# A hybrid decoder step on one core: weight pieces in a ring of four, the last tiles of a pass by quarters, and the base blocks' transposed copy on the vector engine

## The chip, the cores and the metric

One Trainium2 chip, one of its cores. Times are device microseconds (us) of one execution of the whole program. The engines are PE (TensorE, matrix products), DVE (VectorE), ACT (ScalarE), POOL (GpSimd) and SP (SyncE, which here only issues transfers). Each engine works through its own instructions in a fixed order and waits on semaphores where an instruction needs another engine's result. All five can run at once.

## The reference

One layer of a hybrid decoder for a prompt of 1024 tokens and 8 x 8 sample tokens, D_MODEL = 1024. One input projection feeds three groups of heads, whose outputs are joined by one output projection; then an MLP and a gated per-layer embedding.

```python
h = rmsnorm(x, lw['g_mix'])
proj = h @ lw['w_in']
p_rw, p_cv, p_sb = jnp.split(proj, [RW_PROJ, RW_PROJ + 3 * CONV_DIM], axis=-1)
o_rw, wkv_new, shift_new = rwkv7_mixer(p_rw, shift_prev, wkv_prev, lw)
...
q, k, v = [t.reshape(B, T, SB_HEADS, HEAD_DIM) for t in jnp.split(p_sb, 3, axis=-1)]
q = rmsnorm(q, lw['q_gain'])
k = rmsnorm(k, lw['k_gain'])
...
o_sb = stick_breaking(q, k_all, v_all, past_len, lw['sb_bias']).reshape(B, T, SB_DIM)
mixed = jnp.concatenate([o_rw.astype(x.dtype), o_cv.astype(x.dtype), o_sb.astype(x.dtype)], axis=-1)
x = x + mixed @ lw['w_out']
h2 = rmsnorm(x, lw['g_mlp'])
x = x + jnp.square(jax.nn.relu(h2 @ lw['w_up'])) @ lw['w_down']
gate = jax.nn.sigmoid(rmsnorm(x, lw['g_ple']) @ lw['w_ple_gate'])
x = x + gate * (p @ lw['w_ple_proj'])
```

The RWKV group is a recurrence over tokens, `s = s * w + (s a) b^T + v k^T`, `y = s r`, for each of 4 heads. The stick-breaking attention of 8 heads weighs each earlier key with `sigmoid(z)` times the product of `sigmoid(-z)` over the keys between.

## The kernel before

Products are made in fp32 accuracy from two rounded halves: an operand x is split into hi (a copy in the rounded type) and lo (x - hi), and each product is three matmuls, hi by hi, lo by hi and hi by lo. So each weight piece that arrives (tile `wr`, a DMA on SP) is cast by ACT (`wh`, L158) and subtracted by POOL or DVE (`wl`, L159) before PE can use it. `Weights.load` does this for the first stages: RWKV (256 or 128 columns at a time, over all 1024 rows), short conv, and the q, k and v projections of attention (512 columns, as two loads of 512 rows). `wh` and `wl` are two buffers each of a whole load, and `wr` two of one piece of 128x1024.

Stages in the order of the program:

1. Norm and transposes (0 to 45 us), then the RWKV projections (`gemm_t`, L169 to L171) for two pairs of heads j. For the recurrence, each chunk of 64 tokens (prompt) or 8 (sample) gives a triangular matrix: PE makes the products (L260), DVE masks them (`LT`, L262), a DMA lays them out in memory (`l_s`).
2. `wkv_base` inverts the diagonal blocks of these matrices. It loads them (`base_Z`, L278) with a block on each partition, and DVE then runs a loop of two dependent operations for each row (L285 multiplies, L287 adds): 62 operations for the prompt's 32x32 blocks on 128 partitions, 30 for the sample's 16x16 blocks on 16. ACT adds a transposed copy (L288), and SP stores both to `t_s` (L289), from where the later products are loaded as `TT`. The prompt's call stands after the projections of the second pair, the sample's at the head of `wkv_sample_chunk`, which runs at 450 to 580 us.
3. Three passes over eight 128-token tiles make v, q and k (PE at L889), then the prompt's recurrence chunks fill in between. In a pass a tile's 24 matmuls sum into one of two PSUM banks; ACT copies it out (`nat`, L839). In the v pass ACT and POOL split it (`spl`, L850 and L851) and SP stores it (`v_s`, L852), and the plain rows go to the output (L844). The two last tiles (i0 = 6) share the stage with `sample_rows`, which sums the 64 sample rows in one of the same two banks; ACT copies them out in two parts (`nats`, L825 and L826). `spl`, `nats` and the later `st` tiles share one ring of four buffers (tag "st").
4. Short conv, the sample's recurrence chunk and attention A (the first half of the queries), together with the first output projections `out_proj` (L1122 to L1124, groups of twelve matmuls, each group added by DVE at L1424). In attention PE makes the scores (L942, L943), DVE runs the scan (`keep`, L951) and the weighting (`beta`, L953), PE transposes the weights (L971), ACT and DVE split them (`wth`, `wtl`), PE makes the values (L981, L982), and DVE adds the two halves of `o` (L985).
5. Attention B with out_proj and MLP as filling work (from about 597 us), decode attention, the rest of the MLP and the embedding (to the end). PE is full in most of it.

The order on each engine isn't written by hand: the program is written stage by stage, and a list scheduler with a simulated timeline orders each engine's instructions, with `tc.high_priority()` and `tc.issue_after(...)` as hints. So an edit in one place moves instructions elsewhere.

Of the kernel before, what the change touches and what calls it, by code (L numbers as in the profile page):

```python
# [22 lines left out]
F32R = mybir.dt.float32r  # L23
# [25 lines left out]
def hybrid_step(ctx: ExitStack, tc: tile.TileContext, I, O):  # L49
    nc = tc.nc  # L50
    V, S, G, PE, SP = nc.vector, nc.scalar, nc.gpsimd, nc.tensor, nc.sync
# [4 lines left out]
    def f(t):  # L56
        return t.bitcast(F32)
# [36 lines left out]
    l_s = dram.tile([16, 4, 64, 64], F32, name="l_s"), dram.tile([1, 4, 64, 64], F32, name="l_s1")  # L94
    t_s = dram.tile([2, 16, 4, 2, 32, 32], F32, name="t_s"), dram.tile([4, 1, 4, 2, 16, 16], F32, name="t_s1")
# [41 lines left out]
    def P1(name, i=0):  # L137
        return par[:, col[name] + i:col[name] + i + 1]
# [4 lines left out]
    class Weights:  # L143
        def __init__(self, pool):
            self.pool = pool

        def load(self, src, nk=8, ncol=256, tag="w", sub=None):
            wh = self.pool.tile([128, nk * ncol], F32R, name="wh", tag=tag + "h", bufs=2)
            wl = self.pool.tile([128, nk * ncol], F32R, name="wl", tag=tag + "l", bufs=2)
            wh3, wl3 = (w[:, :nk * ncol].rearrange("p (k c) -> p k c", k=nk) for w in (wh, wl))  # L150
            step = max(1, 1024 // ncol)
            for k0 in range(0, nk, step):
                n = min(step, nk - k0)
                raw = self.pool.tile([128, 1024], F32, name="wr", bufs=2)
                r3 = raw[:, :n * ncol].rearrange("p (k c) -> p k c", k=n)
                SP.dma_start(r3, src[k0 * 128:(k0 + n) * 128, :].rearrange("(k p) c -> p k c", p=128))
                flat = slice(k0 * ncol, (k0 + n) * ncol)
                S.copy(wh[:, flat], raw[:, :n * ncol])  # L158
                (sub or (G, G))[k0 // step % 2].tensor_sub(wl[:, flat], raw[:, :n * ncol], f(wh[:, flat]))  # L159
            return wh3, wl3  # L160

    def gemm_t(ps, w, m, x, t0, n, nk=8):

        wh, wl = w
        xh, xl = x
        c = slice(m * 128, m * 128 + 128)
        for k in range(nk):
            a, b = xh[k // 4][:, k % 4, t0:t0 + n], xl[k // 4][:, k % 4, t0:t0 + n]
            PE.matmul(ps[:, :n], wh[:, k, c], a, start=(k == 0), stop=False)  # L169
            PE.matmul(ps[:, :n], wh[:, k, c], b, start=False, stop=False)  # L170
            PE.matmul(ps[:, :n], wl[:, k, c], a, start=False, stop=(k == nk - 1))  # L171

    w_in = I["w_in"][0]
    W = Weights(wpool)
# [6 lines left out]
    for i in range(9):  # L181
# [4 lines left out]
        xt, r = xts[i]  # L186
# [24 lines left out]
    for name, n in rows:  # L211
        src = I[name]
# [56 lines left out]
    def wkv_base(pool, nc_, BS, l_s, t_s, tags=("Z", "X", "Q"), bufs=(1, 1, 1)):  # L269
        na = 64 // BS  # L270
        np_ = nc_ * 4
        P_ = slice(0, na * np_)
        Z = pool.tile([128, BS, BS], F32, name="base_Z", tag=tags[0], bufs=bufs[0])
        X = pool.tile([128, 2, BS, BS], F32, name="base_X", tag=tags[1], bufs=bufs[1])
        Q = pool.tile([128, BS * BS // 4], F32, name="base_Q", tag=tags[2], bufs=bufs[2])
        blocks = l_s.rearrange("c h (a r) (b t) -> a b (c h) r t", a=na, b=na)
        for a in range(na):
            SP.dma_start(Z[a * np_:(a + 1) * np_], blocks[a, a])  # L278
        G.memset(X[P_, 1], 0.0)
        G.memset(X[P_, 1].rearrange("p r t -> p (r t)")[:, 0:BS * BS:BS + 1], 1.0)  # L280

        for j in range(BS - 1):
            n, m = BS - 1 - j, j + 1
            q = Q[P_, 0:n * m].rearrange("p (r c) -> p r c", r=n)
            V.tensor_mul(q, Z[P_, j, m:BS, None].to_broadcast([na * np_, n, m]),  # L285
                         X[P_, 1, None, j, 0:m].to_broadcast([na * np_, n, m]))
            V.tensor_add(X[P_, 1, m:BS, 0:m], X[P_, 1, m:BS, 0:m], q)  # L287
        S.copy(X[P_, 0], X[P_, 1].rearrange("p r t -> p t r"))  # L288
        SP.dma_start(t_s.rearrange("a c h k r t -> (a c h) k r t"), X[P_])  # L289


# [97 lines left out]
    for j in range(2):  # L389
# [312 lines left out]

    def wkv_sample_chunk(bank):
        sp = kp
        wkv_base(kp, 1, 16, l_s[1], t_s[1], ("um", "GS", "um"), (2, 1, 2))
        bm = sp.tile([128, NB, 64], F32, name="bm")
        G.memset(bm, 1.0)
        for s in range(2):
# [89 lines left out]
    def gained(n, flat, r=128):  # L798

        out = sbp.tile([128, 512], F32, name="kg", tag="kg", bufs=2)[:r]  # L800
        G.tensor_mul(*(t.rearrange("p (g d) -> p g d", d=64) for t in (out, flat)),
                     gains[:r, n, None, :].to_broadcast([r, 8, 64]))
        return out

    def products(w):

        for k in range(8):
            hi, lo = (x[k // 4][:, k % 4] for x in w)
            for e, wt in ((0, hi), (0, lo), (1, hi)):
                yield hT[e][k // 4][:, k % 4], wt, k == 0 and e == 0 and wt is hi, k == 7 and e == 1  # L810

    def sample_rows(n, w):

        both = sbp.tile([128, 8, 128], F32R, name="both", tag="nat", bufs=3)
        for e in range(2):
            for g in range(2):
                G.tensor_copy(both[:, 4 * g:4 * g + 4, 64 * e:64 * e + 64], hT[e][g][:, :, NP:T])
        ps = gemm_sb()
        order = [(128, 0)] + [x for k in range(1, 8) for x in ((64, k - 1), (128, k))]
        order[-1:] = [(64, 7), (128, 7)]  # L820
        for m, k in order:
            PE.matmul(ps[:m], both[:, k, :m], w[m == 64][k // 4][:, k % 4], start=(m, k) == (128, 0),
                      stop=(m, k) == (128, 7))
        out, low = (sbp.tile([128, 512], F32, name=f"nats{e}", tag="st", bufs=4)[:64] for e in range(2))
        S.copy(low, ps[64:128])  # L825
        S.copy(out, ps[:64])  # L826
        G.tensor_add(out, out, low)
        if n < 2:
            normed(out, out, NS)
            out = gained(n, out, NS)  # L830
        SP.dma_start(new_s[n], out)
        if n:
            SP.dma_start(outs[n][1][0].rearrange("b j h d -> (b j) (h d)"), out)

    def project(n, ps, i0, nat, i):

        t0 = 128 * (i0 + i)
        flat = nat[:, i]
        S.copy(flat, ps)  # L839
        if n < 2:  # L840
            normed(flat, ps)
        if n:
            out = gained(n, flat) if n == 1 else flat
            SP.dma_start(outs[n][0][0, 0].rearrange("t h d -> t (h d)")[t0:t0 + 128, :], out)  # L844
        if n == 2:
            src = flat.rearrange("p (h d) -> p h d", h=8)
            for hf in range(2):
                hs = slice(4 * hf, 4 * hf + 4)
                spl = sbp.tile([128, 4, 128], F32R, name="spl", tag="st", bufs=4)
                S.copy(spl[:, :, 0:64], src[:, hs])  # L850
                G.tensor_sub(spl[:, :, 64:128], src[:, hs], f(spl[:, :, 0:64]))  # L851
                SP.dma_start(v_s[hs, i0 + i].rearrange("h p e -> p h e"), f(spl))  # L852
# [22 lines left out]
    for n in (2, 0, 1):  # L875
        cols = slice(SB0 + 512 * n, SB0 + 512 * n + 512)
        with tc.high_priority():
            w = tuple(zip(*(W.load(w_in[512 * g:512 * g + 512, cols], nk=4, ncol=512, sub=(G, V)) for g in range(2))))
        for i0 in range(0, 8, 2):
            if i0 == 6:  # L880
                sample_rows(n, w)
            nat = sbp.tile([128, 2, 512], F32, name="nat", tag="nat", bufs=3)
            ps, whole = [None, None], list(products(w))
            for i, part in ((0, whole[:12]), (1, whole[:12]), (0, whole[12:]), (1, whole[12:])) if i0 == 6 else (
                    (0, whole), (1, whole)):
                ps[i] = ps[i] or gemm_sb()
                t0 = 128 * (i0 + i)
                for x, wt, start, stop in part:
                    last = PE.matmul(ps[i], x[:, t0:t0 + 128], wt, start=start, stop=stop)  # L889
# [764 lines left out]
```

## Time and profile before

| | |
|---|---|
| median of 3 runs | 1691.3 us (1691.1 to 1693.27) |
| profiled execution | 1697.94 us, span 1695.9 us |
| mean granted PE clock | 0.988 of full speed |
| busy: PE, DVE, ACT, POOL | 96%, 62%, 47%, 41% |
| moved by DMA | 196.9 MB, 116 GB/s on average |

PE is the engine that is nearly always busy. A change can move the time through PE's idle stretches and its slow ones (the granted clock falls after a stretch of idleness), and through the amount of PE's work, which this change leaves alone. A row of a timeline gives the start, the duration, engine and line, the output and input tiles and their shapes; in brackets stands the engine's idle time before it and what ended that. For a row of several instructions (x3) the duration is the sum's. A row of the windows gives for each engine the busy time in that stretch and its instructions, then the granted clock, the share of the DMA engines and GB/s.

### The profile page before, as it was taken

What the parts mean: (1) busy time and instruction counts of PE and PEld (TensorE: products, weight loads), DVE (VectorE), ACT (ScalarE), POOL (GpSimd) and SP (SyncE); (2) the same over time, 40 slices, a digit from 0 to 9 for tenths busy, and PEclk for the clock granted to TensorE, in tenths of its full rate; (3) what the DMA queues carried; (4) which work ended last, traced back from release to release, by engine and by line L of the source; (5) the groups of instructions that cost most, each with busy time, mean ns of one, the idle gap of its engine ahead of it and who ended that gap; (6) DMA issues with size and microseconds to landing.
All of it is one profiled execution on the core that took longest, in us unless ns stands there. A gap on an engine that the chain in (4) does not pass through costs nothing.

```text
span 1695.9 us, 29332 instructions
## 1 busy us (share of the span) xinstructions
PE 1630.5 (96%) x11229; PEld 1431.9 (84%) x11229; DVE 1054.7 (62%) x1814; ACT 792.1 (47%) x1559; POOL 701.2 (41%) x777
## 2 busy tenths in 40 slices
PE   6999899999998899999999999999999999999998
PEld 5899677778897577888886778988999999999898
DVE  6266644545488679878753335277777677767432
ACT  6544235334267367566543444474444334437421
POOL 4122312123244563333434654366655455538210
PEclk9999999999999899999999999999999999999999
DMA  6044664544246644343344655322322322322211
GB/s 192 27 142 132 174 177 113 137 101 138 71 129 192 167 147 127 105 127 105 92 122 138 186 177 181 122 77 86 99 89 79 96 88 88 96 80 88 72 46 41
DMA packets 201533, 196.92 MB, mean 116 GB/s; under 512 B 58033, under 2 KB 161489, under 8 KB 201266
## 3 DMA queue, kind: packets, MB, share of 16 engines
q1 hardware_dynamic: 189394, 173.52, 34.0%
q0 software_dynamic: 5120, 16.78, 3.3%
q10 hardware_dynamic: 6880, 4.75, 1.1%
q8 instruction: 88, 1.44, 0.3%
q14 instruction: 51, 0.42, 0.1%
HBM read 158.03 MB, written 36.98 MB: 115 GB/s over the span
## 4 chain that ended last, share of the span: by engine, by line
PE 81%; DVE 8%; issue 3%; DMA 3%; ACT 2%; POOL 2%; SPq 1%; ACTq 0%; POOLq 0%; DVEq 0%
PE b L1122 13%; PE b L1124 13%; PE b L1123 13%; PE b L889 6%; PE b L1469 3%; PE b L1471 3%; PE b L1470 3%; PE b L169 3%; PE b L170 3%; PE b L171 3%; DVE keep L951 2%; PE b L971 1%; PE b L524 1%; PE b L981 1%; PE b L1247 1%
## 5 line engine op out<-in xcount | busy, mean ns | idle before, releaser
L1103 POOL TENSOR_TENSOR wl<-wr,wh 128x512 fp32r<-128x512 f32 x172 | 238.7, 1396 | 265.6 <-ACT wh L1102 243.2
L1102 ACT CAST wh<-wr 128x512 fp32r<-128x512 f32 x292 | 179.2, 622 | 298.1 <-PE b L1123 206.3
L1122 PE MATMUL b<-ah,wh 128*128 128x288 f32 (+1 forms) x768 | 254.7, 332 | 5.9 <-DVE x L1509 4.9
L1509 DVE TENSOR_TENSOR x<-b,x 128x288 f32<-128x288 f32 (+1 forms) x384 | 198.4, 528 | 97.0 <-PE b L1124 94.4
L1123 PE MATMUL b<-al,wh 128*128 128x288 f32 (+1 forms) x768 | 252.0, 328 | 0.0
L1124 PE MATMUL b<-ah,wl 128*128 128x288 f32 (+1 forms) x768 | 251.9, 328 | 0.0
L1122 PE MATMUL b<-nh,wh 128*128 128x512 f32 (+1 forms) x448 | 165.8, 371 | 4.4 <-DVE x L1509 1.5
L1123 PE MATMUL b<-nl,wh 128*128 128x512 f32 (+1 forms) x448 | 164.4, 368 | 0.2 <-DVE nl L1346 0.2
L1124 PE MATMUL b<-nh,wl 128*128 128x512 f32 (+1 forms) x448 | 164.2, 367 | 0.0
L1122 PEld LDWEIGHTS b<-ah,wh 128*128 128x128 f32 x768 | 144.6, 188 | 18.4 <-DVE x L1509 8.0
L1123 PEld LDWEIGHTS b<-al,wh 128*128 128x128 f32 x768 | 144.8, 188 | 10.2 <-issue 0.8
L1124 PEld LDWEIGHTS b<-ah,wl 128*128 128x128 f32 x768 | 144.6, 188 | 10.3
L169 PE MATMUL b<-h_hi,wh 128*128 128x384 f32 (+1 forms) x336 | 114.1, 340 | 3.3 <-ACT xs L345 1.3
L170 PE MATMUL b<-h_lo,wh 128*128 128x384 f32 (+1 forms) x336 | 112.6, 335 | 0.3 <-DVE h_lo L201 0.3
L171 PE MATMUL b<-h_hi,wl 128*128 128x384 f32 (+1 forms) x336 | 112.0, 333 | 0.0
L1103 DVE TENSOR_TENSOR wl<-wr,wh 128x512 fp32r<-128x512 f32 x120 | 93.9, 784 | 27.9 <-ACT wh L1102 26.6
L951 DVE TENSOR_TENSOR_SCAN keep<-keep,onesq 128x128 f32<-128x128 f32 (+3 forms) x64 | 97.0, 1515 | 16.5 <-POOL keep L949 16.3
L1122 PEld LDWEIGHTS b<-nh,wh 128*128 128x128 f32 x448 | 84.1, 188 | 18.4 <-DVE x L1424 1.9
L1124 PEld LDWEIGHTS b<-nh,wl 128*128 128x128 f32 x448 | 84.2, 188 | 14.9 <-issue 2.5
L1123 PEld LDWEIGHTS b<-nl,wh 128*128 128x128 f32 x448 | 84.2, 188 | 12.8 <-issue 1.3
L1103 POOL TENSOR_TENSOR wsl<-s,wsh 128x512 fp32r<-128x512 f32 x60 | 77.4, 1313 | 33.1 <-ACT wsh L1102 33.1
L159 POOL TENSOR_TENSOR wl<-wr,wh 128x1024 fp32r<-128x1024 f32 x20 | 48.8, 2449 | 89.2 <-ACT wh L158 89.2
(440 smaller groups left out, 4176.3 us busy)
## 6 DMA issues: line engine op xcount, KB each, us to landing
wr<-in_w_up SPq DMA_DIRECT2D x64, 512.0 KB
wr<-in_w_down SPq DMA_DIRECT2D x64, 512.0 KB
wr<-in_w_in SPq DMA_DIRECT2D x26, 512.0 KB
wr<-in_w_out SPq DMA_DIRECT2D x16, 512.0 KB
xt<-in_x_prompt SPq DMA_DIRECT2D x8, 512.0 KB
v_s<-spl SPq DMA_DIRECT2D x16, 256.0 KB
stk_s<-sth ACTq DMA_DIRECT2D x32, 128.0 KB
stk_s<-stl SPq DMA_DIRECT2D x32, 128.0 KB
```

The lines of the kernel that those rows point to most:

```text
L169: PE.matmul(ps[:, :n], wh[:, k, c], a, start=(k == 0), stop=False)
L170: PE.matmul(ps[:, :n], wh[:, k, c], b, start=False, stop=False)
L171: PE.matmul(ps[:, :n], wl[:, k, c], a, start=False, stop=(k == nk - 1))
L889: last = PE.matmul(ps[i], x[:, t0:t0 + 128], wt, start=start, stop=stop)
L951: V.tensor_tensor_scan(keep[:, 0:L][:, ::-1], keep[:, 0:L][:, ::-1], onesq[:, 0:1].to_broadcast([128, L]), 1.0, op0=ALU.mult, op1=ALU.mult)
L1102: S.copy(h3, src)
L1103: (sub or G).tensor_sub(l3, src, f(h3))
L1122: PE.matmul(ps[:, :n], w(0, k, m), a, start=(k == 0), stop=False)
L1123: PE.matmul(ps[:, :n], w(0, k, m), b, start=False, stop=False)
L1124: PE.matmul(ps[:, :n], w(1, k, m), a, start=False, stop=(k == nk - 1))
L1469: PE.matmul(o, wh[:, k], x[:, 0, k], start=k == 0, stop=False)
L1509: V.tensor_add(p.x[:, m, t0:t0 + n], ps[:, :n], p.x[:, m, t0:t0 + n])
```

## The change

1. `Weights.load` makes a tile for each piece of 1024 columns instead of one for the load, `wh` and `wl` in rings of four. The memory is the same. A load of 512 columns by 1024 rows is four pieces, and a load of 128 columns one.
2. In a pass the two last tiles are written by quarters (six matmuls of one tile, six of the other, and so on) instead of by halves.
3. `wkv_base`'s transposed copy is made by DVE instead of ACT.
4. The sample's `wkv_base` is called right behind the prompt's, with buffers of its own, instead of in `wkv_sample_chunk`.
5. In the v pass the plain rows go out by one DMA for two tiles.

```diff
-            wh = self.pool.tile([128, nk * ncol], F32R, name="wh", tag=tag + "h", bufs=2)
-            wl = self.pool.tile([128, nk * ncol], F32R, name="wl", tag=tag + "l", bufs=2)
...
+                hi, lo = (self.pool.tile([128, 1024], F32R, name=f"w{e}", bufs=4) for e in "hl")
+                hi, lo, raw = (t[:, :n * ncol] for t in (hi, lo, raw))
+                S.copy(hi, raw)
+                sub[k0 // step % 2].tensor_sub(lo, raw, f(hi))
+                for e, t in enumerate((hi, lo)):
+                    w[e].extend(t[:, k * ncol:k * ncol + ncol] for k in range(n))
...
-        S.copy(X[P_, 0], X[P_, 1].rearrange("p r t -> p t r"))
+        V.tensor_copy(X[P_, 0], X[P_, 1].rearrange("p r t -> p t r"))
         SP.dma_start(t_s.rearrange("a c h k r t -> (a c h) k r t"), X[P_])
...
             wkv_base(bp, 16, 32, l_s[0], t_s[0])
+            wkv_base(bp, 1, 16, l_s[1], t_s[1], ("Zs", "Xs", "Qs"))
...
     def wkv_sample_chunk(bank):
         sp = kp
-        wkv_base(kp, 1, 16, l_s[1], t_s[1], ("um", "GS", "um"), (2, 1, 2))
...
-        if n:
-            out = gained(n, flat) if n == 1 else flat
-            SP.dma_start(outs[n][0][0, 0].rearrange("t h d -> t (h d)")[t0:t0 + 128, :], out)
+        to = outs[n][0][0, 0].rearrange("t h d -> t (h d)") if n else None
+        if n == 1:
+            SP.dma_start(to[t0:t0 + 128, :], gained(n, flat))
+        if n == 2 and i:
+            SP.dma_start(to[t0 - 128:t0 + 128, :].rearrange("(i p) c -> p i c", p=128), nat)
...
-            w = tuple(zip(*(W.load(w_in[512 * g:512 * g + 512, cols], nk=4, ncol=512, sub=(G, V)) for g in range(2))))
+            w = W.load(w_in[:, cols], ncol=512, sub=(G, V))
...
-            for i, part in ((0, whole[:12]), (1, whole[:12]), (0, whole[12:]), (1, whole[12:])) if i0 == 6 else (
+            for i, part in [(i, whole[6 * q:6 * q + 6]) for q in range(4) for i in range(2)] if i0 == 6 else (
                     (0, whole), (1, whole)):
```

The lines behind the change move by two to four: L288 becomes L290, L289 becomes L291, L825 and L826 become L827 and L828, L850 and L852 become L854 and L856, L985 becomes L989, L1424 becomes L1428.

The edit moves instructions at several places. SP's queue where the base blocks are loaded, before (l_s are the stores of the masked matrices, out the last rows of the shift state, bk_s a store of a recurrence operand; l_s_73 is the sample's):

```order
L265 DMA l_s<-LT_1326 64x8x64
L265 DMA l_s_73<-LT_1333 64x64
L461 DMA out<-last 1x1024
L444 DMA bk_s<-pinv 128x1088
L462 DMA out<-last 8x1024
L278 DMA base_Z<-l_s 64x32x32 x2
```

and after:

```order
L267 DMA l_s<-LT_1328 64x8x64
L267 DMA l_s_73<-LT_1335 64x64
L154 DMA wr<-in_w_in 128x2x512
L280 DMA base_Z<-l_s 64x32x32 x2
L280 DMA base_Z<-l_s_73 4x16x16 x4
L447 DMA bk_s<-pinv 128x1088
L458 DMA ar_s<-xs 128x1088
L464 DMA out<-last 1x1024
```

The base blocks' loads, of prompt and sample, now stand ahead of three stores. SP's queue where the prompt's base block is stored, before (each v_s row is the two stores of one tile; ar, bk and TT are loads for the recurrence; wr are the q pass's last two weight pieces):

```order
L844 DMA out<-nat 128x512
L852 DMA v_s<-spl 128x4x128 x2
L844 DMA out<-nat 128x512
L289 DMA t_s<-base_X 128x2048
L852 DMA v_s<-spl 128x4x128 x2
L499 DMA ar<-ar_s 128x3x64 x2
L502 DMA ar<-ar_s 128x2x64 x3
```

and after:

```order
L291 DMA t_s_75<-base_X 16x512
L856 DMA v_s<-spl 128x4x128 x2
L848 DMA out<-nat 128x2x512
L856 DMA v_s<-spl 128x4x128 x2
L291 DMA t_s<-base_X 128x2048
L856 DMA v_s<-spl 128x4x128 x2
L848 DMA out<-nat 128x2x512
L502 DMA ar<-ar_s 128x3x64 x2
```

Before, the stores of tile 4 stand ahead of t_s and those of tile 5 behind it; after, those of tile 4 stand behind it. ACT's order at the same place, before:

```order
L839 COPY nat<-b_3289 128x512
L288 COPY base_X<-base_X 128x1024
L850 CAST spl<-nat 128x4x64 x2
L825 COPY nats_3347<-b_3329 64x512
L826 COPY nats_3346<-b_3329 64x512
```

and after:

```order
L841 COPY nat<-b_3333 128x512
L854 CAST spl<-nat 128x4x64 x2
L827 COPY nats_3391<-b_3373 64x512
L828 COPY nats_3390<-b_3373 64x512
L841 COPY nat<-b_3398 128x512
```

The transposed copy is gone from ACT. DVE's order after, at the head of the base blocks (128-partition rows are the prompt's, 16-partition rows the sample's):

```order
L287 TENSOR_TENSOR base_Q<-base_Z,base_X 128x87
L287 TENSOR_TENSOR base_Q<-base_Z,base_X 16x39
L289 TENSOR_TENSOR base_X<-base_X,base_Q 128x29x3
L289 TENSOR_TENSOR base_X<-base_X,base_Q 16x13x3
L462 TENSOR_TENSOR xs<-b_1660,xs 128x384
L287 TENSOR_TENSOR base_Q<-base_Z,base_X 128x112
L287 TENSOR_TENSOR base_Q<-base_Z,base_X 16x48
```

The two blocks' operations alternate, and a multiplication that stood ahead of the base block stands between them. DVE's order at the end of attention A, before (L755, L763 and L764 belong to the sample's chunk, `wtl` and `o` to attention, L1424 to out_proj):

```order
L755 TENSOR_TENSOR FTs<-b_4592,id_378 128x512
L763 TENSOR_TENSOR GS<-b_4609,GS 128x512
L985 TENSOR_TENSOR o_6084<-b_6069,o_6084 64x256
L764 TENSOR_TENSOR GS<-GS,pcs 128x512
L61 TENSOR_TENSOR wtl<-b_6102,wth 128x256
L61 TENSOR_TENSOR wtl<-b_6102,wth 128x128
L985 TENSOR_TENSOR o_6116<-b_6088,o_6116 64x256
L1424 TENSOR_TENSOR x<-b_6254,x 128x512
L1424 TENSOR_TENSOR x<-b_6268,x 128x512
```

and after:

```order
L61 TENSOR_TENSOR wtl<-b_6105,wth 128x512
L1428 TENSOR_TENSOR x<-b_6346,x 128x512
L989 TENSOR_TENSOR o_6100<-b_6085,o_6100 64x256
L61 TENSOR_TENSOR wtl<-b_6118,wth 128x256
L1428 TENSOR_TENSOR x<-b_6298,x 128x512
L61 TENSOR_TENSOR wtl<-b_6118,wth 128x128
L1428 TENSOR_TENSOR x<-b_6374,x 128x512
L989 TENSOR_TENSOR o_6132<-b_6104,o_6132 64x256
L1428 TENSOR_TENSOR x<-b_6360,x 128x512
```

The sample's operations have moved ahead of this piece, and additions of out_proj stand between the last values of attention A.

More of the change, by code (lines that the diff above doesn't have):

```diff
@@ L145, in __init__, with load @@
             self.pool = pool
-        def load(self, src, nk=8, ncol=256, tag="w", sub=None):
-            wh = self.pool.tile([128, nk * ncol], F32R, name="wh", tag=tag + "h", bufs=2)
-            wl = self.pool.tile([128, nk * ncol], F32R, name="wl", tag=tag + "l", bufs=2)
-            wh3, wl3 = (w[:, :nk * ncol].rearrange("p (k c) -> p k c", k=nk) for w in (wh, wl))
+        def load(self, src, nk=8, ncol=256, sub=(G, G)):
+            w = [], []
             step = max(1, 1024 // ncol)
@@ L154, in load @@
                 raw = self.pool.tile([128, 1024], F32, name="wr", bufs=2)
[L155 to L160, printed above, removed]
+                SP.dma_start(raw[:, :n * ncol].rearrange("p (k c) -> p k c", k=n),
+                             src[k0 * 128:(k0 + n) * 128, :].rearrange("(k p) c -> p k c", p=128))
+                hi, lo = (self.pool.tile([128, 1024], F32R, name=f"w{e}", bufs=4) for e in "hl")
[4 more added lines that the diff above has]
+                    w[e].extend(t[:, k * ncol:k * ncol + ncol] for k in range(n))
+            return w
     def gemm_t(ps, w, m, x, t0, n, nk=8):
@@ L168, in gemm_t @@
             a, b = xh[k // 4][:, k % 4, t0:t0 + n], xl[k // 4][:, k % 4, t0:t0 + n]
-            PE.matmul(ps[:, :n], wh[:, k, c], a, start=(k == 0), stop=False)
-            PE.matmul(ps[:, :n], wh[:, k, c], b, start=False, stop=False)
-            PE.matmul(ps[:, :n], wl[:, k, c], a, start=False, stop=(k == nk - 1))
+            PE.matmul(ps[:, :n], wh[k][:, c], a, start=(k == 0), stop=False)
+            PE.matmul(ps[:, :n], wh[k][:, c], b, start=False, stop=False)
+            PE.matmul(ps[:, :n], wl[k][:, c], a, start=False, stop=(k == nk - 1))
     w_in = I["w_in"][0]
@@ L807, in products @@
         for k in range(8):
-            hi, lo = (x[k // 4][:, k % 4] for x in w)
+            hi, lo = w[0][k], w[1][k]
             for e, wt in ((0, hi), (0, lo), (1, hi)):
@@ L821, in sample_rows @@
         for m, k in order:
-            PE.matmul(ps[:m], both[:, k, :m], w[m == 64][k // 4][:, k % 4], start=(m, k) == (128, 0),
+            PE.matmul(ps[:m], both[:, k, :m], w[m == 64][k], start=(m, k) == (128, 0),
                       stop=(m, k) == (128, 7))
```

## The prediction

> **What bounds the kernel now.** I read the page's busy shares first, then the stages as windows, then what TensorE (PE) waits for in the stages that are not full, then the timelines of the engines named there. The forecast is a difference: the profiled execution took 1697.94 us (span 1695.9), the median of the timed runs is 1691.3 us, 6.6 us less; I sum the gains and losses on the profiled execution and take them off the median.
>
> ```profile
> PE 1630.5 (96%) x11229; PEld 1431.9 (84%) x11229; DVE 1054.7 (62%) x1814; ACT 792.1 (47%) x1559; POOL 701.2 (41%) x777
> ```
>
> ```profile
> 192.00:240.00 48.00, 38.81 (x213) 29.91 (x212) 21.59 (x46) 16.13 (x26) 11.61 (x11) 0.93 0.55 148
> 240.00:465.00 225.00, 221.53 (x2082) 179.67 (x2081) 114.09 (x247) 84.73 (x171) 58.01 (x62) 1.00 0.44 115
> 465.00:527.00 62.00, 62.00 (x520) 58.56 (x520) 51.43 (x111) 36.31 (x88) 23.32 (x71) 0.97 0.43 130
> 527.00:577.00 50.00, 41.69 (x290) 26.44 (x288) 39.74 (x66) 33.29 (x74) 27.31 (x42) 0.86 0.63 194
> 577.00:600.00 23.00, 18.96 (x78) 14.54 (x78) 12.48 (x43) 5.63 (x11) 9.39 (x11) 0.93 0.86 232
> ```
>
> PE is busy 96% of the span, so there are 65 us to win in all, and only where PE is idle or runs at a low granted clock (in a window's row the number behind the five engines' busy times). The change touches two such places. The first is 192 to 240 us, the end of the v pass: 9.2 us idle, clock 0.93. The second is 527 to 600 us, the end of attention A: 12.3 us idle (50 - 41.69 and 23 - 18.96) and, at clocks of 0.86 and 0.93, about 41.69 x 0.14 + 18.96 x 0.07 = 7.2 us of slow work. Between them PE is full, so what is won early is kept.
>
> Place one, by PE's waits and by the timelines of PE, ACT, DVE and SP's queue:
>
> ```profile
> PE b L889 <- ACT nats L826: 5.9, 1, 5.9
> ```
>
> ```profile
> 208.35 0.80 PE L889 MATMUL b<-wh,h_hi 128*128 128x512 f32 x1 [5.93 <-ACT nats L826]
> ...
> 212.35 0.44 PE L889 MATMUL b<-wh,h_hi 128*128 128x512 f32 x1
> ...
> 213.54 0.39 PE L889 MATMUL b<-wh,h_lo 128*128 128x512 f32 x1
> 213.77 0.39 PE L889 MATMUL b<-wh,h_hi 128*128 128x512 f32 x1
> ```
>
> ```profile
> 227.80 0.50 PE L889 MATMUL b<-wl,h_hi 128*128 128x512 f32 x1 [1.71 <-POOL wl L159]
> ```
>
> ```profile
> 204.55 1.93 ACT L288 COPY base_X<-base_X 128x1024 f32<-128x1024 f32 x1 [10.67 <-DVE base_X L287]
> ...
> 207.72 0.58 ACT L826 COPY nats<-b 64x512 f32<-64x512 f32 x1
> ...
> 211.36 0.40 ACT L850 CAST spl<-nat 128x256 fp32r<-128x256 f32 x1 [1.27 <-DMA v_s<-spl]
> ```
>
> ```profile
> 158.28 2.62 DVE L159 TENSOR_TENSOR wl<-wr,wh 128x1024 fp32r<-128x1024 f32 x1 [1.35 <-ACT wh L158]
> 161.41 1.41 DVE L262 TENSOR_TENSOR LT<-b,mfull 128x512 f32<-128x512 f32 x3
> 170.32 1.67 DVE L459 TENSOR_TENSOR xs<-b,xs 128x384 f32<-128x384 f32 x3 [3.65 <-PE b L458]
> 176.43 0.19 DVE L285 TENSOR_TENSOR base_Q<-base_Z,base_X 128x31 f32<-128x31 f32 x1 [4.44 <-DMA base_Z<-l_s]
> ...
> 192.41 0.43 DVE L285 TENSOR_TENSOR base_Q<-base_Z,base_X 128x256 f32<-128x256 f32 x1
> ...
> 204.32 0.19 DVE L287 TENSOR_TENSOR base_X<-base_X,base_Q 128x31 f32<-128x31 f32 x1
> ```
>
> ```profile
> 166.96 0.30 SPq L461 DMA_DIRECT2D out<-last  x1
> 168.28 0.34 SPq L444 DMA_DIRECT2D bk_s<-pinv  x1
> 170.36 1.92 SPq L278 DMA_DIRECT2D base_Z<-l_s  x2
> ...
> 206.50 0.33 SPq L289 DMA_DIRECT2D t_s<-base_X  x1
> 207.61 1.73 SPq L852 DMA_DIRECT2D v_s<-spl  x2
> ...
> 220.12 0.93 SPq L156 DMA_DIRECT2D wr<-in_w_in  x2
> ```
>
> The 62 dependent DVE operations of the prompt's base block run from 176.43 to 204.51. ACT's transposed copy L288 stands in ACT's order ahead of the evictions L825 and L826 of the sample rows' bank, so ACT sits idle for 10.67 us, and PE's last tile, which needs that bank, starts at 208.35. The restart is slow: 4.00 us for nine matmuls to 212.35, 0.43 each, against 0.23 between 213.54 and 213.77, so 1.8 us more. Then the q pass lacks its last two weight pieces (wr issued at 220.12, behind the ar, bk and TT loads); the lo half comes at 227.80.
>
> **The change at place one.** *The copy.* On DVE it leaves ACT's queue; ACT's evictions now follow the spl casts, so the 5.93 us wait for ACT as such is gone. But SP's order above now has the store t_s ahead of tile 4's two v_s stores, where it stood behind them. The nats tiles share a four-buffer ring with spl, and their evictions must wait until those v_s stores have landed. So what is late next is SP: it waits at t_s for the DVE copy, and behind it are v_s, the evictions and PE's last tile. Call T the issue of t_s. In the trace the second of two v_s stores behind t_s has released its cast at 211.36, which is T + 4.86 with T = 206.50; an eviction of 0.58 behind that makes the tile start at T + 5.5. Before it started at T + 1.85. The stall is handed from ACT to SP, not removed, and all hangs on how much earlier T comes.
>
> *T.* The LT products (L262) move ahead of the v weights' 2.62 us subtraction on DVE, 68 matmuls of L260 eleven products (2.5 us) earlier on PE, and base_Z's load now stands ahead of the stores that in the trace went out from 166.96 on: the load goes out 3 us (161.41 to 158.3) to 4.4 us earlier; I take 3.9, and the chain starts at 176.43 - 3.9 = 172.5. Its first 30 operations took 16.0 us (to 192.41), its last 32 took 12.1. New in it: three multiplications L459, 1.67 us less the gaps they fill, 1.4; the sample's own copy, 0.3 (an estimate: ACT's 0.65 for 16x256, less by the ratio of the two engines' casts, all shown below); the large copy; and 30 small operations of the sample's base block, one after each large one. Their price is bounded by rows of place two, where they ran before:
>
> ```profile
> 460.99 0.21 DVE L285 TENSOR_TENSOR base_Q<-base_Z,base_X 16x63 f32<-16x63 f32 x1
> 461.13 1.35 DVE L1045 SCALAR_TENSOR_TENSOR cc<-ue,par,cc 128x1104 f32<-128x1104 f32 x1
> 462.41 0.20 DVE L287 TENSOR_TENSOR base_X<-base_X,base_Q 16x63 f32<-16x63 f32 x1
> ...
> 463.82 0.20 DVE L285 TENSOR_TENSOR base_Q<-base_Z,base_X 16x64 f32<-16x64 f32 x1
> 464.06 0.21 DVE L287 TENSOR_TENSOR base_X<-base_X,base_Q 16x64 f32<-16x64 f32 x1
> ```
>
> Dependent, they start 0.24 apart (463.82, 464.06). Beside independent work the neighbour starts 0.14 after (460.99, 461.13), and the next one 0.07 before that neighbour's end (462.41 against 462.48). Between two dependent large operations, which lie 0.03 apart, a small one then costs 0.14 - 0.07 - 0.03 = 0.04: 30 x 0.04 = 1.1 us, at full price 30 x 0.24 = 7.2 us. I take 1.1, since that is the arrangement of the order. The large copy isn't in the trace; its bounds are the DVE cast of as many elements, 0.69, and ACT's 1.93 for the same transposed shape (ns of the shortest, median and longest of a line):
>
> ```profile
> L411 DVE CAST rb<-rk x4: 220/458/694, 93.2 to 138.4; 128x1024 fp32r<-128x1024 f32 x2, 128x128 fp32r<-128x128 f32 x2
> L158 ACT CAST wh<-wr x26: 1039/1048/1074, 12.9 to 445.1; 128x1024 fp32r<-128x1024 f32 x26
> L288 ACT COPY base_X<-base_X x2: 647/1287/1927, 204.5 to 469.5; 128x1024 f32<-128x1024 f32 x1, 16x256 f32<-16x256 f32 x1
> ```
>
> ACT's plain cast of 128x1024 takes 1.04, so the transposed shape costs ACT 1.9 times as much; 0.69 x 1.9 = 1.3, which I take. T = 172.5 + 16.0 + 12.1 + 1.4 + 0.3 + 1.1 + 1.3 = 204.7. The Trainium skill, "VectorE: DVE Perf Modes", the perf-mode tier table, gives an fp32 tensor_copy 1227 ns for 2048 elements, by estimate 0.6 for this one: T and the sum would be 0.7 earlier; no row of before shows it.
>
> *The result of place one.* The last tile starts at 204.7 + 5.5 = 210.2, 1.9 later. What PE meets next are the q pieces: SP has 28 issues behind t_s ahead of them instead of 21, one out store for two tiles instead of one for each being the only saving; at the 13.6 us that the 21 took, T + 13.6 to T + 17, I take T + 15.4 = 220.1, as before. So the lo half again comes at 227.8, the two waits trade places, and place one gives 0: bounds -6 (T at 210.8) to +4 (T at 200.7). The ring of pieces itself I cost at nothing: before 192 us PE waits for no weights, and in a 512-column pass four pieces are in flight in both kernels. The quarters of the last two tiles too: PE's order starts the last tile only after the first, as before.
>
> **The change at place two.** The sample's base block leaves DVE here (30 operations, most of them up to 0.21 us, some 6 in all, ACT's 0.65, two trips to memory), so the sample's products are done earlier and their bank is free for out_proj (L1122 to L1124). Counted in the two orders from the last conv product to attention B's first score: 84 out_proj matmuls before, 24 of them ahead of attention A's last value product; 132 after, 92 of them ahead. So 68 move into the stretch in which PE idles and the clock sinks, and 48 more are done by the start of attention B: 48 x 0.227 = 10.9 us of work taken out of the full stage behind. From this goes what the start of attention B comes later:
>
> ```profile
> 577.72 0.43 DVE L985 TENSOR_TENSOR o<-b,o 64x256 f32<-64x256 f32 x1 [1.25 <-ACT o L984]
> 578.67 1.29 DVE L1424 TENSOR_TENSOR x<-b,x 128x512 f32<-128x512 f32 x2 [0.52 <-ACT x L1332]
> 579.87 0.21 DVE L1164 TENSOR_SCALAR qm_i<-qi 128x1 int32<-128x1 int32 x2
> ...
> 584.53 0.15 DVE L1175 TENSOR_TENSOR bits<-bits,bits 128x1 f32<-128x1 f32 x1
> ...
> 588.76 3.98 DVE L1197 TENSOR_TENSOR biases<-biases 128x8 f32<-128x8 f32 x1
> ```
>
> DVE's order now has seven L1424 additions (0.65 each), the 29 small operations of the decode set-up (2.6 us in the trace, two stretches between 579.87 and 584.68) and L1197 (3.98) ahead of attention A's last `o`, where they stood behind it. With each row of the order at its duration in the trace, DVE's work up to the thirteenth of the sixteen `o` is the same in both (the sample's operations out, two additions in); from there to the last it is 7.0 us before and 16.4 now, 9.4 more. DVE is idle for 10 of the 50 us in 527 to 577, so part of it fits into gaps, and the neighbours of L1197 with its 128x8 shape take 0.2, so that its 3.98 need not come again. The last `o` comes 0 to 9.4 us later; I take 4. The gate behind it, mix_s, mixl, bias, keeps its length. Gain 10.9 - 4 = 7, bounds 1.5 and 11. Sum: 0 + 7; 1691.3 - 7 = 1684.3.
>
> **Rivals.** *A. The stall is really gone.* If T came before 199, tile 4's stores would land before PE needs the bank, and the 9.2 us of idle time and the 1.8 us of slow matmuls go: 11 + 7, 1673. For it: base_Z goes out earlier. Against: it needs 6 us more than my sum finds. *B. The sample's operations at full price.* T = 204.7 + 6.1 = 210.8, the pieces come 6 us later, and the gain of place two is eaten: 1690, no change. Against it speak the rows at 461.13 and 462.41. The Trainium skill, "VectorE: DVE Perf Modes", section "The DRAIN you can't avoid", says that a next operation starts only when the pipe is empty, which would make B the forecast; the rows with starts 0.07 before the end disagree, and the page's section on two instructions with no wait between them allows that. A tail that returns most of place two's gain ends at the same time. *C. Slower: out_proj and attention A take turns.* PE runs in order; if each group of twelve out_proj matmuls holds up the value products behind it while DVE waits for them, the 68 don't overlap: 15.4 us, less 20 fewer behind the last `o` (4.5), plus 5.6 of DVE work (9.4 without L1197's long stay), so attention B starts 16.5 later, 5.6 us lost: 1697. It decides from 14.3 us later on (10.9 + 3.4). For it: in 527 to 577 each engine waits for the others; against: PE has 8 us idle there.
>
> **How the numbers follow.** Forecast, 1684 (own range 1677 to 1688): 0.50. A 0.12; B and the eaten gain 0.21; C, or a T so late that it costs more than place two gives, 0.17. 0.2%, about what a measurement of this kernel can tell from no change, is 3.4 us: faster 0.62, same 0.21, slower 0.17. The range runs from near A to C's time, 1674 to 1697.
>
> **What would show it.** In the trace after: no copy on ACT, the evictions waiting for v_s; PE's last v tile near 210; t_s near 204.7; the sample's operations 0.04 dear; 527 to 600 with a clock over 0.93 and more out_proj ahead of the last `o`. Wrong would be: a last tile before 205 (A), t_s at 210 (B), or attention B starting 14 us later (C).

## The result and the profile after

The changed kernel took 1679.86 us (median of 4 runs, 1677.24 to 1682.75), the kernel before 1691.2 in the same series; the ratio is 0.9932 (95% interval 0.9912 to 0.9952), 11.3 us less. The forecast was 1684.3, with 1677 to 1688 as its own range. The profiled execution after has a span of 1681.0 us.

One measure that the page does not give is needed first. All kernels here run the same matmuls. *Lost time* up to a point is the time at which PE starts a certain matmul, less what all matmuls ahead of it in PE's order take at the spacing that each shape has in full stretches (0.227 us for 128x512). It counts idle time and slow clock, wherever the order has put the work. The spacings are read off dense stretches of these traces, so only differences between kernels mean something. Where a column ends depends on the matmul taken as the mark: taken a few us earlier or later, it moves some 3 us between the columns 240-390 and 390-700, while their sum stays within about 1 us. Lost in each stretch, us, worked out from the timelines of PE:

| kernel | to 165 | 165-240 | 240-390 | 390-700 | 700-865 | 865-1050 | 1050-1500 |
|---|---|---|---|---|---|---|---|
| before, first profile | 34.9 | 14.3 | 41.4 | 72.3 | 3.8 | 26.5 | 14.5 |
| before, second profile | 36.7 | 15.2 | 41.7 | 72.5 | 3.8 | 19.7 | 16.0 |
| after | 39.2 | 15.0 | 37.0 | 62.6 | 4.1 | 20.9 | 14.6 |

Against the second profile: nothing at place one (165 to 240), 4.7 us won right behind it, 9.9 us won at place two (390 to 700), 2.5 us lost at the start, where two profiles of the same kernel differ by 1.8.

Place one and place two after. The windows, then of place one PE's two waits, ACT's evictions and SP's queue:

```profile
192.00:240.00 48.00, 39.08 (x210) 30.18 (x209) 20.24 (x41) 14.43 (x24) 11.80 (x12) 0.89 0.66 180
465.00:527.00 62.00, 61.77 (x482) 56.44 (x481) 46.03 (x93) 35.52 (x81) 23.36 (x63) 0.97 0.45 129
527.00:577.00 50.00, 39.34 (x304) 29.73 (x305) 42.46 (x87) 33.81 (x77) 32.48 (x53) 0.93 0.73 225
577.00:600.00 23.00, 22.00 (x110) 18.29 (x109) 12.71 (x32) 6.98 (x16) 10.00 (x12) 1.00 0.51 148
```

The stretch between the places, in the first profile before and then after:

```profile
390.00:465.00 75.00, 71.53 (x625) 62.67 (x624) 39.25 (x91) 22.77 (x43) 23.80 (x27) 1.00 0.40 109
```

```profile
390.00:465.00 75.00, 73.69 (x738) 64.47 (x737) 34.80 (x72) 23.77 (x48) 24.37 (x25) 1.00 0.35 94
```

```profile
213.11 0.79 PE L893 MATMUL b<-wh,h_hi 128*128 128x512 f32 x1 [6.32 <-ACT nats L828]
229.75 0.55 PE L893 MATMUL b<-wh,h_hi 128*128 128x512 f32 x1 [2.61 <-ACT wh L158]
```

```profile
211.55 0.58 ACT L827 COPY nats<-b 64x512 f32<-64x512 f32 x1 [12.24 <-DMA v_s<-spl]
212.48 0.58 ACT L828 COPY nats<-b 64x512 f32<-64x512 f32 x1 [0.35 <-DMA v_s<-spl]
```

```profile
206.47 0.34 SPq L291 DMA_DIRECT2D t_s<-base_X  x1
206.90 1.46 SPq L856 DMA_DIRECT2D v_s<-spl  x2
...
224.42 0.91 SPq L154 DMA_DIRECT2D wr<-in_w_in  x2
```

The transposed copy is gone from ACT, and ACT's evictions now wait 12.24 us for v_s, which SP issues behind t_s: the wait before PE's last tile is 6.32 us where it was 5.93. The q pieces go out at 224.42 instead of 220.12.

DVE's chain, with POOL beside it, and three rows of before:

```profile
173.47 0.19 DVE L287 TENSOR_TENSOR base_Q<-base_Z,base_X 128x31 f32<-128x31 f32 x1 [2.12 <-DMA base_Z<-l_s]
...
180.22 0.49 DVE L287 TENSOR_TENSOR base_Q<-base_Z,base_X 128x207 f32<-128x207 f32 x2
180.63 1.04 DVE L289 TENSOR_TENSOR base_X<-base_X,base_Q 128x207 f32<-128x207 f32 x2
181.60 1.04 DVE L287 TENSOR_TENSOR base_Q<-base_Z,base_X 128x220 f32<-128x220 f32 x2
...
191.00 0.41 DVE L287 TENSOR_TENSOR base_Q<-base_Z,base_X 128x256 f32<-128x256 f32 x1
...
205.32 1.12 DVE L290 COPY base_X<-base_X 128x1024 f32<-128x1024 f32 x1
```

```profile
180.78 5.71 POOL L855 TENSOR_TENSOR spl<-nat,spl 128x256 fp32r<-128x256 f32 x6 [30.41 <-ACT spl L854]
```

```profile
184.69 0.37 DVE L285 TENSOR_TENSOR base_Q<-base_Z,base_X 128x207 f32<-128x207 f32 x1
185.10 0.80 DVE L287 TENSOR_TENSOR base_X<-base_X,base_Q 128x207 f32<-128x207 f32 x1
185.93 0.46 DVE L285 TENSOR_TENSOR base_Q<-base_Z,base_X 128x220 f32<-128x220 f32 x1
```

A large and a small operation together (x2) start 0.41 us ahead of the next pair (180.22, 180.63); in before the large one alone takes the same 0.41 (184.69, 185.10). The sample's operation costs nothing there. Beside POOL's subtractions it costs about 0.1 us: the next pair of that size starts 0.97 us ahead of its follower (180.63, 181.60), the large one alone 0.83 (185.10, 185.93; POOL subtracts there too).

Place two after: PE's longest wait, two scans of the same size on DVE with what POOL does beside the second, L1201 with POOL's subtractions, attention A's last `o`, attention B's first score, and before's first score:

```profile
567.42 0.88 PE L975 MATMUL b<-ident,beta 128*128 128x128 f32 x3 [6.66 <-DVE wtl L61]
```

```profile
545.60 1.23 DVE L955 TENSOR_TENSOR_SCAN keep<-keep,onesq 128x512 f32<-128x512 f32 x1
...
564.81 2.29 DVE L955 TENSOR_TENSOR_SCAN keep<-keep,onesq 128x512 f32<-128x512 f32 x1 [1.07 <-POOL keep L953]
```

```profile
564.74 3.41 POOL L1107 TENSOR_TENSOR wl<-wr,wh 128x512 fp32r<-128x512 f32 x2
```

```profile
579.24 3.03 DVE L1201 TENSOR_TENSOR biases<-biases 128x8 f32<-128x8 f32 x1
...
591.91 0.43 DVE L989 TENSOR_TENSOR o<-b,o 64x256 f32<-64x256 f32 x1 [2.38 <-ACT o L988]
```

```profile
579.71 2.53 POOL L1107 TENSOR_TENSOR wl<-wr,wh 128x512 fp32r<-128x512 f32 x2
```

```profile
602.29 0.53 PE L946 MATMUL b<-stk_k,stk_q 128*128 128x512 f32 x2 [1.64 <-DMA stk_q<-stk_s]
```

```profile
598.46 0.39 PE L942 MATMUL b<-stk_k,stk_q 128*128 128x512 f32 x1
```

Attention B's first score comes 3.8 us later than in the first profile before (0.4 later than in the second, where it stands at 601.86), with 48 more out_proj matmuls done by then. In 577 to 600 PE is busy for 22.00 of 23 us at a clock of 1.00, against 18.96 at 0.93. Over 527 to 600 its idle time hardly changed, 12.3 us before and 11.7 after; what fell is the slow work, by the prediction's formula from 7.2 us to 39.34 x 0.07 = 2.8.

### The profile page after: what moved, and what is told of

It is laid out like the page before. It is cut to its first block, busy times and chain, and to the rows that moved or that the text cites. A ratio compares the mean times of both kernels' runs of the same rounds, so it can differ in the third digit from the quotient of the medians.

```text
span 1681.0 us, 29326 instructions
## 1 busy us (share of the span) xinstructions
PE 1622.1 (96%) x11229; PEld 1430.4 (85%) x11229; DVE 1051.9 (63%) x1816; ACT 789.6 (47%) x1557; POOL 706.2 (42%) x777
## 5 line engine op out<-in xcount | busy, mean ns | idle before, releaser
L1107 POOL TENSOR_TENSOR wl<-wr,wh 128x512 fp32r<-128x512 f32 x172 | 243.2, 1423 | 263.4 <-ACT wh L1106 229.7
L1107 DVE TENSOR_TENSOR wl<-wr,wh 128x512 fp32r<-128x512 f32 x120 | 96.5, 806 | 29.4 <-ACT wh L1106 28.7
L1107 POOL TENSOR_TENSOR wsl<-s,wsh 128x512 fp32r<-128x512 f32 x60 | 77.3, 1309 | 35.1 <-ACT wsh L1106 35.1
L893 PE MATMUL b<-wh,h_hi 128*128 128x512 f32 x192 | 78.9, 412 | 8.9 <-ACT nats L828 6.3
```

The source lines that it names most:

```text
L1107: (sub or G).tensor_sub(l3, src, f(h3))
```

## Experiments

Ratios are to the kernel before, on the same chip and in the same series. "Counts a/b" are out_proj matmuls in PE's order ahead of attention A's last value product and by attention B's first score: before 24/84, after 92/132. In the first two series the medians of before were 1693.2 and 1693.4 us, in the third 1699.9. The three series ran on three chips, and the third (`early_quarters`, `quarters`, `ring`, `dve_copy`) has no profile of before, so lost times of its kernels are compared across chips.

**Undoing or doing the early base block.** `late_sample`, the changed kernel with the sample's base block late again (24/72):

```diff
-            wkv_base(bp, 1, 16, l_s[1], t_s[1], ("Zs", "Xs", "Qs"))
...
         sp = kp
+        wkv_base(kp, 1, 16, l_s[1], t_s[1], ("um", "GS", "um"), (2, 1, 2))
```

> The changed kernel with one part undone: the sample's base block is made in wkv_sample_chunk again. Out_proj matmuls ahead of attention A's last value product: 24 (as before the change; 92 in the changed kernel), 72 by attention B's first score (84 before, 132 changed). Theory 1 (the gain is out_proj work that fills attention A's end, because the sample's chain is done earlier): the gain is lost, 1688 to 1696 us, ratio to before 0.998 to 1.003. Rival (the weight ring, the quarters or the copy on DVE bring it): about 1680, ratio 0.993.

Measured 1685.11 us, 0.9959 (0.9944 to 0.9974): neither. By the medians the early base block is worth about 0.27% on top of the rest (the two intervals overlap), and the rest has a gain of its own, which I had put at nothing.

`only_early`, the kernel before with those two lines moved the other way (46/96):

> The kernel before with one part of the change alone: the sample's base block is made early, with the copy on ACT, the old weight buffers and halves. Out_proj matmuls ahead of attention A's last value product: 46, 96 by attention B's first score. Theory 1 with the gain proportional to the out_proj work done by attention B's start (12 more matmuls, 2.7 us): 1687 to 1690, ratio 0.998 to 0.999. Rival 2 (what counts is that the sample's operations leave DVE there, whatever out_proj does): about 1681 to 1684, ratio 0.994 to 0.996. If the rest of the change brings the gain: 1691.

Measured 1700.81 us, 1.0049 (1.0035 to 1.0063): slower, which no theory had. The same edit gains in one neighbourhood and costs in another. Its trace shows where: DVE's last `o`, PE's first score.

```profile
590.39 0.43 DVE L985 TENSOR_TENSOR o<-b,o 64x256 f32<-64x256 f32 x1
```

```profile
602.51 0.53 PE L942 MATMUL b<-stk_k,stk_q 128*128 128x512 f32 x2 [1.66 <-DMA stk_q<-stk_s]
```

The last `o` and the first score come as late as in the changed kernel (DVE's order has decode set-up and additions ahead of that `o` here too), but with 96 out_proj matmuls done instead of 132. It loses 75.2 us in 390 to 700 (72.5 before) and 10.1 in 700 to 865 (3.8). So theory 1', made after this run and tested below: not where the base block is computed, but the order of out_proj that comes of it decides.

`act_copy`, the changed kernel with the copies on ACT (92/132):

```diff
-        V.tensor_copy(X[P_, 0], X[P_, 1].rearrange("p r t -> p t r"))
+        S.copy(X[P_, 0], X[P_, 1].rearrange("p r t -> p t r"))
```

> The changed kernel with the transposed copies on ACT again. At place two its order has the same counts as the changed kernel (92 and 132). Theory 1: place two keeps its gain, and place one was worth nothing, so 1677 to 1683, ratio 0.991 to 0.996. Rival (taking the copy off ACT is part of the gain): 1684 to 1690, ratio 0.996 to 0.999.

Measured 1681.35 us, 0.9931 (0.9915 to 0.9947), like the changed kernel: a part of the copy on DVE in the gain, if any, is below the 0.2% that this measurement can tell.

`ring_only`, ring, quarters and paired store without the other two parts (24/72):

> The kernel before with the ring of pieces, the quarters and the paired output store alone; copy on ACT, sample's base block late. Out_proj counts 24 and 72. Theory 1: no gain, 1688 to 1695, ratio 0.998 to 1.002. Rival (the ring and the quarters bring the gain): about 1680 to 1685, ratio 0.993 to 0.996.

Measured 1686.98 us, 0.9967 (0.9955 to 0.9979): a small gain, between both expectations.

**A second profile of before.** `before_again`, unchanged:

> The kernel before, unchanged, for a second profile. In the first one, PE lost 5 to 8 us more between 865 and 1050 us (decode attention) than in each of the five other kernels profiled so far, and that execution was 4 to 6 us over the median of its timed runs. Theory: that loss was this one execution's; the second profile has a span of 1688 to 1692 us and loses 5 us less there. Rival: the change moves the decode's order too and the gain is real; the loss comes again, span about 1695.

The span is 1693.7 us, 1.7 above the theory's range, and PE lost 19.7 us in 865 to 1050 (first profile 26.5; after 20.9). The loss didn't come again, so that difference of the traces is no part of the change. The windows of the first and the second profile:

```profile
865.00:1050.00 185.00, 179.25 (x1211) 136.81 (x1210) 77.91 (x114) 74.73 (x138) 95.12 (x92) 0.99 0.52 158
```

```profile
865.00:1050.00 185.00, 183.46 (x1248) 140.80 (x1247) 84.04 (x122) 78.30 (x144) 96.70 (x94) 1.00 0.55 165
```

But it isn't shown to be one execution's. PE is busy there for 178.7 to 179.4 us in the first profile and in all four kernels of the third series, and for 182.4 to 184.4 in the second profile, in the changed kernel and in all kernels of the first two series. So the loss goes with the series, and so perhaps with the chip, whatever the kernel; why stays open.

**The test of the out_proj theory.** `hold_out_proj`, the changed kernel with out_proj's first half held back (0/96):

```diff
-    out_proj(A, 0, 4)
+    with tc.issue_after(last_value[0].ins):
+        out_proj(A, 0, 4)
```

(`last_value` is set by attention's L986.)

> The changed kernel, with the first half of out_proj for tokens 0 to 511 (96 matmuls) ordered behind attention A's last value product: 0 ahead of it instead of 92, 96 by attention B's first score instead of 132. Theory 1 (out_proj matmuls that fill the end of attention A are the gain): 36 matmuls (8.2 us) later than in the changed kernel and 12 more than before by attention B's start, with PE idle longer in 530 to 580: 1688 to 1694 us, ratio 0.997 to 1.001. Rival (the gain is that the sample's chain is shorter and attention A ends earlier): 1678 to 1684, ratio 0.992 to 0.996.

Measured 1696.29 us, 1.002 (1.0007 to 1.0033): just above the forecast range: the whole gain and a little more is gone. Not all else is as in the changed kernel, since the scheduler reorders around the edit: of 16.0 us more lost in 390 to 865, about 10 lie in 390 to 700 and about 6 behind it, in 700 to 865, where PE is busy 160.90 of 165 us here and all 165 in the changed kernel. PE's waits in 527 to 600, of this kernel:

```profile
PE b L987 <- DVE o L991: 9.2, 5, 3.3
PE b L1128 <- DVE x L1430: 2.4, 1, 2.4
```

PE stands there behind DVE's `o`, with nothing to fill the time: in 527 to 577 it is busy 37.18 us at a clock of 0.83, after the change 39.34 at 0.93.

`early_copy`, the kernel before with the early base block and the copies on DVE (46/96, the edits of `only_early` and of `dve_copy`):

> The kernel before with two parts of the change: the sample's base block early and the copies on DVE; old weight buffers, halves. Out_proj counts 46 ahead of attention A's last value product, 96 by attention B's first score, as with the early base block alone (which was slower, 1700.8). Theory 1' (what the early base block brings depends on how much out_proj the order puts ahead of attention A's last values, and the copy does nothing): again slower than before, 1696 to 1703, ratio 1.002 to 1.006. Rival (the early base block is good only with the copy on DVE, since on ACT it blocks that queue for two copies): 1681 to 1688, ratio 0.993 to 0.997.

Measured 1702.41 us, 1.0058 (1.0041 to 1.0075): slower again, as theory 1' has it.

`early_quarters`, the kernel before with the early base block and the quarters (90/132):

```diff
-            for i, part in ((0, whole[:12]), (1, whole[:12]), (0, whole[12:]), (1, whole[12:])) if i0 == 6 else (
+            for i, part in [(i, whole[6 * q:6 * q + 6]) for q in range(4) for i in range(2)] if i0 == 6 else (
```

> The kernel before with two parts of the change: the sample's base block early, and the last two tiles of a pass by quarters; old weight buffers, copies on ACT, a store for each tile. Its order has 90 out_proj matmuls ahead of attention A's last value product and 132 by attention B's first score, where the early base block alone has 46 and 96. Theory 1' (the time at place two follows these counts, whichever edit makes the scheduler come to them): 1680 to 1686 us, ratio 0.993 to 0.997. Rival (the early base block costs time unless the weight ring is there): 1696 to 1703, ratio 1.002 to 1.006.

Measured 1689.85 us against 1699.87, 0.994 (0.9923 to 0.9958): the forecast ratio. One line turns a loss of 0.5% into a gain of 0.6%, and with it the scheduler comes to 90/132.

**The parts alone.** `quarters`, that one line (24/84):

> The kernel before with the quarters alone. Counts 24 and 84, as before the change. Ring, quarters and paired store together (without the early base block) gave 0.9967. Theory: that came from the ring (loads of a pass in four pieces), so the quarters alone give 1691 to 1695, ratio 0.999 to 1.001. Rival: it came from the quarters, 1685 to 1689, ratio 0.996 to 0.998.

Measured 1698.25 us, 0.9993 (0.9982 to 1.0005): nothing that can be told from no change.

`ring`, the new `load` alone (24/72):

> The kernel before with the weight pieces in a ring of four alone: halves, copies on ACT, base block late, a store for each tile. Counts 24 and 72. Theory: the ring carries what ring, quarters and paired store gave together: 1685 to 1689, ratio 0.996 to 0.998. Rival: the quarters carry it: 1691 to 1695, ratio 0.999 to 1.001.

Measured 1695.4 us, 0.9977 (0.9964 to 0.9989): by the medians the ring carries most of what ring, quarters and paired store give together (the intervals overlap).

`dve_copy`, the copies on DVE alone (24/84):

> The kernel before with the copies on DVE alone. In its order the v_s stores of tile 4 stay ahead of t_s, so the wait for ACT is gone and nothing on SP takes its place. Theory (from the run with nats tiles of their own, where PE's wait moved to the first recurrence chunk): the last v tile starts at 203, and PE waits 6 to 9 us at the first chunk or at the q pieces instead: 1690 to 1696, ratio 0.998 to 1.002. Rival (the stall of 5.9 us and its cold restart were the loss): 1684 to 1688, ratio 0.994 to 0.997.

Measured 1697.11 us, 0.9989 (0.9978 to 1.0). The eviction's wait is gone, PE goes on through the last v tile, and stands 8.60 us later:

```profile
213.74 1.33 PE L524 MATMUL b<-ar,bk 64*128 64x128 f32 x8 [8.60 <-DMA bk<-bk_s]
```

**Freeing place one.** `nats_wr`, the changed kernel with other buffers for the v pass's nats and the q pieces on ACT's queue (93/132):

```diff
-        out, low = (sbp.tile([128, 512], F32, name=f"nats{e}", tag="st", bufs=4)[:64] for e in range(2))
+        out, low = (sbp.tile([128, 512], F32, name=f"nats{e}", **(dict(tag="kg", bufs=2) if n == 2 else dict(tag="st", bufs=4)))[:64] for e in range(2))
...
-            w = W.load(w_in[:, cols], ncol=512, sub=(G, V))
+            w = W.load(w_in[:, cols], ncol=512, sub=(G, V), q=S if n == 0 else SP)
```

(`q`, the queue that issues the piece, is a new argument of `load`, SP by default.)

> The changed kernel with two edits at place one: the v pass's nats tiles get two buffers of another ring, so that the sample rows' eviction needn't wait for the v_s stores behind t_s, and the q pass's weight pieces are issued on ACT's queue instead of SP's, so that they don't queue behind the ar, bk and TT loads. Theory 1 (place one is worth 0 in the changed kernel because SP's queue gates first the eviction and then the q pieces): the last v tile starts at 203 to 206 instead of 213, the lo half of the third q piece is there by 222 instead of 231, and the time falls by 5 to 9 us: 1671 to 1676, ratio 0.988 to 0.991. Rival (the pieces wait for buffers or PE, not for the queue): 1679 to 1682, ratio 0.993 to 0.995.

Measured 1685.8 us, 0.9955 (0.9938 to 0.9971): no gain over the changed kernel. ACT's first eviction, PE's wait:

```profile
199.72 0.59 ACT L827 COPY nats<-b 64x512 f32<-64x512 f32 x1 [1.35 <-PE b L824]
```

```profile
217.44 1.28 PE L527 MATMUL b<-ar,bk 64*128 64x128 f32 x8 [8.21 <-DVE wl L159]
```

The evictions come 11.8 us earlier and wait for PE alone, and PE's last v tile doesn't wait. PE then stops for 8.21 us at the first recurrence chunk. The profile puts that wait down to DVE's last operation, but the matmul reads ar and bk, and SP issued the first bk load at 215.27, 2.2 us before it starts; in `dve_copy` the same load went out at 211.45, 2.3 us before PE's start at 213.74. So in both kernels the stall went to the next work that hangs on what SP loads behind t_s. The q pieces gained nothing on ACT's queue: they went out at 223.11, 1.3 us earlier than in the changed kernel, though ACT does nothing in the 9.77 us before 224.53. What held them stays open.

All profiles, by counts, with the time lost in 390 to 865:

| counts | kernels: lost, us |
|---|---|
| 90/132 to 93/132 | after 66.7, act_copy 65.7, nats_wr 68.6, early_quarters 70.4 |
| 24/72 | ring_only 69.3, ring 73.7, late_sample 73.9 |
| 24/84 | before 76.1 and 76.3, quarters 76.2, dve_copy 75.5 |
| 46/96 and 0/96 | early_copy 82.7, hold_out_proj 82.7, only_early 85.3 |

Kernels with the same counts lie roughly together, whatever parts they have, though the first two rows meet (70.4 and 69.3). The counts are a mark of the order and not a scale: 46/96 is worse than 24/84. Why the three worst lose 6 us more in 700 to 865, I did not test; in all three PE waits 3.1 or 3.2 us for DVE's `o` in 700 to 880, in the changed kernel not at all.

## Why the prediction was right

**The stall is handed from ACT to SP: right.** The copy left ACT, the evictions wait for v_s behind t_s, and place one gave 0.2 us for a forecast 0. `dve_copy` and `nats_wr` show more: the stall belongs to neither wait. In both it moves on to the next consumer of what SP loads behind DVE's chain (8.60 and 8.21 us).

**T: 204.7 forecast, 206.47 measured.** The chain started at 173.47 (172.5). Its first 30 operations with the sample's 30 and the three multiplications took 17.5 us (18.5 by the terms). The sample's operations cost nothing each while POOL is idle and about 0.1 beside POOL, where I had 0.04 each and rival B 0.24. The rule of the Trainium skill, "VectorE: DVE Perf Modes", section "The DRAIN you can't avoid", that a next operation starts only when the pipe is empty, isn't what this trace shows (0.41 us for a pair as for the large one alone); the section itself lets a next operation that isn't held start earlier. The large copy took 1.12 (1.3 by the row's ratio; the estimate from the same page's table was 0.6). The term too small was the last 32 operations: 12.1 forecast, 14.3 measured from 191.00 to 205.32, of which the sample's copy, moved in among them, takes 0.5. The rest is four operations that took twice their usual time, 1.7 us in all, from 195.52 on and from 198.94 on, each while POOL's L855 subtracted (195.27 to 196.95 and 198.82 to 200.39); before, POOL is idle from 190.72 to 206.86. The sum had no term for POOL.

**Behind T: sized too small twice.** PE's tile started at T + 6.6 (I had 5.5), since the second v_s landed later. The q pieces went out at T + 18.0 (I had 15.4 out of 13.6 to 17): past the upper bound. Neither cost what it seems, since PE had recurrence chunks to run meanwhile.

**Place two: right in sum, wrong inside.** 48 matmuls more by attention B's first score, 10.9 us, and a later start of 4 us were forecast; measured are 3.8 by the clock of the first profile, and 5.2 counted from the last conv product, from which the forecast counts (525.91 before, 524.57 after). But the last `o` came 14.2 us later, beyond my bound of 9.4, and the gate behind it took 10.4 us instead of the 20.7 of before. I had said that it keeps its length. In before most of that gate was out_proj work itself (60 matmuls, 13.6 us) and DVE's set-up, which in the changed order lies ahead of the `o`: two errors of opposite sign, and that they cancel is luck.

The picture behind the sum was wrong too. The 68 matmuls (15.4 us) were to fill PE's idle time at the end of attention A. But the last value product came 14.3 us later (576.88 before, 591.20 after), and PE's idle time in 527 to 600 went from 12.3 to 11.7 us only: out_proj and attention A did take turns, as rival C has it. C's loss didn't come, because the gate became shorter by 10.3 us and the clock stayed higher. The longest wait left, 6.66 us, stands behind a scan on DVE that takes 2.29 us beside POOL's subtractions and 1.23 without.

The gain, 7 forecast, was 9.9 by lost time in 390 to 700. About 2 of it lie ahead of place two: in 390 to 465 PE idles 3.5 us before (with waits of 1.4 for DVE's `FT`, L595, and 1.1 for ACT's `cc`, L1016) and 1.3 after. `hold_out_proj`, which takes the out_proj work out of attention A, loses about 10 us again in 390 to 700; with `early_quarters` it shows that the order there carries the gain.

**Missed: 240 to 390.** 4.7 us were won where I had put nothing. The profiles with quarters lose 37.0 to 39.3 us there, those without 41.4 to 42.4; `nats_wr` (42.3) is an exception: PE waits there 2.8 us for DVE's `nat` (L798). PE shows no waits there in the kernels before and after, so the cause stays open, and the timing of `quarters` alone (0.9993) doesn't confirm a gain of that size. Of the parts that I costed at nothing, the ring is worth 0.2%; its mechanism was not isolated.

**What I could not have known from the diff:** that the sign of the early base block's effect hangs on a neighbouring edit. The forecast rested on the counts of the changed order, not on the edit, and the counts held in the runs that tested them.

## What to carry to other kernels

When a scheduler orders the instructions, cost the order, not the edit: the same move cost 0.5% in one neighbourhood and, with one line more, gained 0.6%. Before removing a wait, ask what the waiting engine needs next and who delivers it; if that hangs on the same chain, the stall moves on. And compare kernels by lost time at equal work, with two profiles of the baseline, before explaining a stage: one of the largest differences of the two traces, 6 us in decode, was no part of the change and showed again in every kernel of another series.

## What the runs showed of the hardware

Some DVE operations slow beside POOL's subtractions. The pair of 128x207 at 180.22 takes 0.49 us, the next one of that size 1.04 while POOL's L855 runs (180.78 to 186.49), and the scan of 128x512 takes 1.23 us without POOL's L1107 and 2.29 beside it. Not all slow: `wtl` of 128x512, which reads PSUM, takes 0.69 us both beside L1107 (at 569.19) and mostly clear of it (at 584.10). L1201, a multiplication of 128x8, ended at 582.27, with POOL's L1107 at 582.24, after 3.03 us; in `act_copy` the same operation, with POOL not subtracting, took

```profile
574.56 0.17 DVE L1201 TENSOR_TENSOR biases<-biases 128x8 f32<-128x8 f32 x1
```

So the 3.98 us of the profile before were no price of that operation; there too it ended, at 592.74, with POOL's subtractions (L1103, at 592.71). Small independent DVE operations in the gaps of a dependent chain were free while POOL was idle, and cost about 0.1 us each beside its subtractions.
